# One running sum of probability tiles in the attention stage of a hybrid attention and recurrence layer

## The chip, the core and the metric

The kernel runs on one core of a Trainium2 chip. The metric is the device time of one execution in microseconds (us). The engines of the core work in parallel, each through its own instructions in a fixed order, and wait for one another by semaphores: TensorE (PE) multiplies matrices, VectorE (DVE), ScalarE (ACT) and GpSimd (POOL) work on elements, and SyncE (SP) issues the transfers between the memory outside the core and its own. SBUF is the memory on the core that all engines read. PSUM, in banks, takes what TensorE produces.

## The reference

One layer takes 2048 latent tokens of width 1024 and 256 context tokens. After a modulated RMS norm one projection feeds two groups of heads, whose outputs are concatenated and projected again; a SwiGLU feed-forward part follows. The change concerns the attention group alone:

```python
def latent_attention(qx, kx, vx, kc, vc):        # 8 query heads, 2 key/value heads, head_dim 64
    keys = jnp.concatenate([kc, kx], axis=1)     # 256 + 2048 = 2304 keys
    vals = jnp.concatenate([vc, vx], axis=1)
    def block(q):                                # 128 queries at a time
        s = jnp.einsum('bqkgd,bnkd->bkgqn', q, keys).astype(jnp.float32) * scale
        p = jax.nn.softmax(s, axis=-1)
        return jnp.einsum('bkgqn,bnkd->bqkgd', p.astype(vals.dtype), vals)
```

So for each query the kernel needs the largest score, the sum of the exponentials over 2304 keys, and the exponentials times the values. The other group is a gated linear recurrence over the same tokens.

## The kernel before

The program runs in stages: modulation and projections, then attention and recurrence together, the output projection, and the feed-forward part in two halves. The change touches the second of these.

**Items.** Attention is cut into 32 items (class `Item`): 16 blocks of 128 queries for each of the 2 key/value heads. An item holds 4 query heads of 128 queries, so 512 columns, against 18 key tiles of 128 keys (`NKT`). The loop over `x` counts key tiles of all items in turn: step `k` of item `n` is `x = 18 n + k`.

**A step** does three things. `scores` multiplies one key tile with the 512 query columns in two matrix products (lines 1096 and 1097: `qa` with the keys `K`, then a second one with the low parts and the maximum, `qb` with `KB`), and ScalarE writes the exponential into half of a pair tile `p` of 128 by 1024 (line 1100), so that an item has 9 pairs, 0 to 8. Beside it `chunk` works for the NEXT item: one more matrix product (`mx`, line 1065, or two halves at line 1071) whose row minima VectorE reduces into `mn` (lines 1067 and 1073). The score is kept negated, so the minimum gives the maximum. A bank for `mx` comes from a pool of two, `ps_mx`.

**The maxima.** After the last chunk VectorE reduces `mn` to `neg`, 128 by 4 (line 1077). At step 10 `maxima` transposes it on TensorE into a bank of `ps_mx` (`pn`, line 1082), ScalarE copies 4 rows of it, and they go into the next item's `qb`.

**The two events.** At step 10 (the first event, pairs 0 to 3) and at step 2 of the item after (the second event, pairs 4 to 8) TensorE leaves the scores and runs a batch: `pa`, the recurrence's products (line 724), and then `av`, values times exponentials (line 1121, column halves of 64). After that the sums over the keys are made: a pair of 128 by 1024 is multiplied with `one32`, 32 columns of ones, in 8 small matrix products (line 1129), which add up in columns 256 to 383 of `av`. A matrix product in float32 stands as two records in the trace, so 8 of them are 16 records. The banks of `av` are copied out at step 3 (`drain`), the sums inverted at step 10 (`invert`, line 1139) and applied at step 13 (`finish`, `pb` and `oo`).

**The sums.** Not every pair is multiplied with ones. A table `SUMS = ".PEP.PPE."` has a letter for each pair: a dot opens a group that is multiplied with ones, P is added to its group by GpSimd as soon as the pair is there, E is added by VectorE in the event. So pairs 0 to 3 become one tile `ps` in the first event, 4 to 7 another in the second, and pair 8 is multiplied by itself. An item has 4 additions on GpSimd, 2 on VectorE (all at line 1111) and 3 times 8 products with ones. The tile `ps` has one buffer (`op`, bufs=1).

**The recurrence** runs alongside. In each event, `rec.round()` yields the `pa` products and then one level of its work: VectorE's `copy_predicated` into `A` (line 737), ScalarE's `M`, GpSimd's `M`, `Q` and `C` (lines 753, 758 and 761). VectorE also makes the decay products `T` (line 779) after the event.

**The order.** In this stage TensorE, VectorE, ScalarE and GpSimd run in the order in which the code is written (`manual_schedule`); only SP's queue is left to the scheduler after the first item. A wait at the head of an engine therefore holds everything behind it.

## Time and profile before

| | us |
|---|---|
| median of 3 runs | 3124.36 |
| lowest and highest run | 3119.69, 3128.83 |
| span of the profiled execution | 3122.6 |
| stage of the items in it, from 731.51 to 1635.50 | 904.0 |
| mean granted TensorE clock | 0.996 |

A row of a timeline reads: start in us from the span's start, length in us, engine, line, operation, what it writes and reads, shape, number of instructions merged, and in brackets the engine's idle time before it with what ended it. A row of the chain of waits reads: start, length, engine, what, count; it is the work that the end hangs on. A row of groups reads: what, count | busy time, mean of one in ns | idle time before, by what ended it. Matrix products are pipelined and overlap in these rows, so the time that one costs is seen from the distance between starts. GpSimd's spans are rough.

### The profile page before, as it was taken

What the parts mean: (1) busy time and instruction counts of PE and PEld (TensorE: products, weight loads), DVE (VectorE), ACT (ScalarE), POOL (GpSimd) and SP (SyncE); (2) the same over time, 40 slices, a digit from 0 to 9 for tenths busy, and PEclk for the clock granted to TensorE, in tenths of its full rate; (3) what the DMA queues carried; (4) which work ended last, traced back from release to release, by engine and by line L of the source; (5) the groups of instructions that cost most, each with busy time, mean ns of one, the idle gap of its engine ahead of it and who ended that gap; (6) DMA issues with size and microseconds to landing.
All of it is one profiled execution on the core that took longest, in us unless ns stands there. A gap on an engine that the chain in (4) does not pass through costs nothing.

```text
span 3122.6 us, 51024 instructions
## 1 busy us (share of the span) xinstructions
PE 3069.2 (98%) x18732; PEld 2472.9 (79%) x18732; DVE 1863.3 (60%) x3234; ACT 1302.1 (42%) x2656; POOL 1647.5 (53%) x1302
## 2 busy tenths in 40 slices
PE   7999999999999999999999999999999999999998
PEld 5888888887777778777778878888878788888887
DVE  5554665526787786787745574544468844333567
ACT  4422332314455555455553243333345533333454
POOL 3422232205998888898862118776600177676122
PEclk9999999999999999999999999999999999999999
DMA  8343455425111222111124344656495533332755
GB/s 286 101 148 118 142 150 161 140 72 140 42 35 48 65 55 72 40 46 54 42 76 154 116 155 155 212 175 213 169 329 191 188 114 109 102 101 101 253 195 196
DMA packets 374789, 410.75 MB, mean 132 GB/s; under 512 B 36261, under 2 KB 265865, under 8 KB 374026
## 3 DMA queue, kind: packets, MB, share of 16 engines
q1 hardware_dynamic: 374538, 407.49, 40.9%
q8 instruction: 147, 2.41, 0.3%
q14 instruction: 104, 0.85, 0.1%
HBM read 277.54 MB, written 133.97 MB: 132 GB/s over the span
## 4 chain that ended last, share of the span: by engine, by line
PE 82%; DVE 6%; DMA 2%; POOL 2%; issue 1%; ACT 1%; SPq 0%; POOLq 0%; ACTq 0%; DVEq 0%
PE pA L1685 14%; PE pB L1685 7%; PE av L1121 7%; PE f L346 6%; PE y L1261 6%; PE pd0A L1982 4%; PE s L1096 3%; PE pC L1685 3%; PE pd1A L1982 3%; PE s L1097 3%; PE mx L1065 3%; DVE mn L1067 2%; PE i L353 2%; PE pd0B L1982 2%; PE pd1B L1982 2%; PE pa L724 2%
## 5 line engine op out<-in xcount | busy, mean ns | idle before, releaser
L1100 ACT ACTIVATE p<-s 128x512 f32<-128x512 f32 x576 | 337.8, 600 | 375.3 <-PE s L1097 361.4
L1067 DVE TENSOR_REDUCE mn<-mx 128x1 f32<-128x512 f32 x496 | 336.9, 689 | 176.4 <-PE mx L1065 173.7
L1121 PE MATMUL av<-p,VS 128*64 128x256 f32 x2304 | 259.9, 380 | 0.0
L1096 PE MATMUL s<-qa,K 128*128 128x512 f32 x576 | 244.7, 425 | 1.1 <-ACT p L1100 1.0
L1097 PE MATMUL s<-qb,KB 128*128 128x512 f32 x576 | 227.4, 395 | 0.0
L1121 PEld LDWEIGHTS av<-p,VS 128*64 128x64 f32 x2304 | 160.4, 137 | 75.2 <-issue 1.1
L1111 POOL TENSOR_TENSOR ps<-p,p 128x1024 f32<-128x1024 f32 x64 | 153.2, 2394 | 104.5 <-ACT p L1100 104.4
L1065 PE MATMUL mx<-K,qa 128*128 128x512 f32 x496 | 199.7, 403 | 2.7 <-DVE mn L1067 1.4
L346 PE MATMUL f<-hTh,wh 128*128 128x512 f32 (+1 forms) x640 | 187.8, 373 | 0.0
L1111 POOL TENSOR_TENSOR ps<-ps,p 128x1024 f32<-128x1024 f32 x64 | 153.0, 2391 | 11.9 <-ACT p L1100 10.6
L1919 DVE TENSOR_TENSOR dl<-dl,x 128x512 fp32r<-128x512 f32 x154 | 113.4, 760 | 68.1 <-ACT x L1912 63.9
L1912 ACT ACTIVATE x<-dl 128x512 fp32r<-128x512 f32 x154 | 96.2, 632 | 97.0 <-DMA dl<-s_hid0S 39.2
L758 POOL TENSOR_TENSOR Q<-Q,T 128x512 f32<-128x512 f32 x96 | 129.2, 1362 | 8.1 <-PE pa L724 7.7
L346 PEld LDWEIGHTS f<-hTh,wh 128*128 128x128 f32 x640 | 116.2, 189 | 20.0 <-DVE ge L361 0.2
L1912 ACT ACTIVATE dh<-dl 128x512 fp32r<-128x512 f32 x154 | 89.0, 624 | 101.5 <-PE pd1A L1982 44.7
L1919 DVE TENSOR_TENSOR dl<-dl,dh 128x512 fp32r<-128x512 f32 x154 | 105.5, 698 | 42.7 <-ACT dh L1912 40.4
L1096 PEld LDWEIGHTS s<-qa,K 128*128 128x128 f32 x576 | 109.3, 190 | 26.7 <-issue 12.3
L123 POOL TENSOR_TENSOR rs_xf<-ms_xf,mhalf 128x1 f32<-128x1 f32 x16 | 9.8, 617 | 223.5 <-DVE ms_xf L121 221.5
L1065 PEld LDWEIGHTS mx<-K,qa 128*128 128x128 f32 x496 | 93.7, 189 | 38.2 <-DVE mn L1067 15.3
L1097 PEld LDWEIGHTS s<-qb,KB 128*128 128x128 f32 x576 | 109.6, 190 | 14.8 <-issue 0.2
L346 PE MATMUL f<-hTl,wh 128*128 128x512 f32 (+1 forms) x320 | 118.0, 369 | 0.0
L1949 POOL TENSOR_TENSOR y<-y,yg 128x512 f32<-128x512 f32 x24 | 40.5, 1704 | 145.0 <-DVE yg L1948 118.0
(435 smaller groups left out, 8961.8 us busy)
## 6 DMA issues: line engine op xcount, KB each, us to landing
w<-in_w_gu_dram SPq DMA_DIRECT2D x88, 512.0 KB
wm<-in_w_mod_dram SPq DMA_DIRECT2D x24, 1024.0 KB
dl<-s_wT SPq DMA_DIRECT2D x88, 256.0 KB
dl<-s_wB SPq DMA_DIRECT2D x66, 256.0 KB
wq<-in_w_down_dram SPq DMA_DIRECT2D x44, 256.0 KB
s_wT<-wq SPq DMA_DIRECT2D x44, 256.0 KB
dl<-s_hid1S SPq DMA_DIRECT2D x44, 256.0 KB
dl<-s_hid0S SPq DMA_DIRECT2D x44, 256.0 KB
```

The source lines that it names most:

```text
L346: nc.tensor.matmul(pm[:, :n], w[wi][:, k, c0:c0 + P], hT[b][hi][:, k, :], start=(k == 0 and i == 0), stop=(k == KT - 1 and i == 2))
L1065: nc.tensor.matmul(s, self.qa[:, h * P:(h + 1) * P], K[:, k * 512:(k + 1) * 512], start=True, stop=True)
L1067: nc.vector.tensor_reduce(self.mn[:, h, k:k + 1], s, axis=AX.X, op=ALU.min)
L1096: nc.tensor.matmul(s, KS[self.g][:, ks], self.qa, start=True, stop=False)
L1097: nc.tensor.matmul(s, KB[k // 6][:, k % 6 * P:(k % 6 + 1) * P], self.qb, start=False, stop=True)
L1100: nc.scalar.activation(self.pairs[p][:, o:o + 512], s, AF.Exp, scale=-1.0)
L1111: (nc.gpsimd if SUMS[p] in "PQ" else nc.vector).tensor_tensor(t, a, self.pairs[p], op=ALU.add)
L1121: nc.tensor.matmul(self.av[i * 64:(i + 1) * 64, :256], VS[k // 6][:, k % 6, :], self.pairs[k // 2][:, o:o + 256], start=(k == 0), stop=(k ...
L1261: nc.tensor.matmul(py, m[:, k, :], wo[k][w][hf], start=(k == 0 and i == 0), stop=(k == KT - 1 and i == 2), skip_group_check=True)
L1685: nc.tensor.matmul(acc, w[wi][:, k, :], x[xi][k], start=(start and k == 0 and i == 0), stop=(stop and k == KH - 1 and i == 2), skip_group_ ...
L1919: nc.vector.tensor_tensor(lo, f32v(lo), f32v(hi), op=ALU.subtract)
L1982: nc.tensor.matmul(cur[t], l[:, t * P:(t + 1) * P], r, start=(start and j == 0 and f == 0), stop=(stop and j == NHF - 1 and f == 2), skip_ ...
```

## The change

`SUMS` and its groups go. An item has one tile `ps`, and every pair is added to it: pairs 1, 3, 5 and 6 by GpSimd when they are there (`POOL_ADDS`), pairs 2 and 4 by VectorE in the first event and 7 and 8 in the second (`DVE_ADDS`). The first of VectorE's two additions stands where its one stood, before the recurrence's level, the other after the level. The products with ones are made once per item, in the second event. GpSimd's addition of pair 5 now continues the sum that VectorE left, where it began a new tile before.

`neg` becomes one tile of 128 by 128 for all items, zero outside its first 4 columns, and all 128 columns are transposed. `smapad` takes the place in `sma` that the old `neg` tiles had.

```diff
--- before.py
+++ after.py
@@ -620,6 +620,7 @@
         kvp = pool(st, "kvp", 1, side="right")
         qpl = pool(st, "qpl", 1, side="right")
         sm = pool(st, "sma", 3, side="right")
+        sm.tile([P, 24], F32, name="smapad", bufs=1)
         pp = pool(st, "pp", 8, side="right")
         op = pool(st, "op", 1, side="right")
         ps_st = pool(st, "ps_st", 3, PSUM, side="right")
@@ -1041,7 +1042,7 @@
             def __init__(self, n, qt, g):
                 self.n, self.qt, self.g = n, qt, g
                 self.nm = f"{qt}_{g}"
-                self.pairs, self.sums, self.av = {}, {}, None
+                self.pairs, self.sum, self.av = {}, None, None
 
             def load(self):
                 self.qa = qpl.tile([P, 512], F32R, tag="qa", name=f"qa{self.nm}", bufs=3)
@@ -1073,13 +1074,12 @@
                     nc.vector.tensor_reduce(self.mn[:, h:h + 2, 4], s.rearrange("p (h k) -> p h k", h=2),
                                             axis=AX.X, op=ALU.min)
                 if c == 17:
-                    self.neg = sm.tile([P, 4], F32, tag="neg", name=f"neg{self.nm}")
-                    nc.vector.tensor_reduce(self.neg, self.mn, axis=AX.X, op=ALU.min)
+                    nc.vector.tensor_reduce(neg[:, :4], self.mn, axis=AX.X, op=ALU.min)
 
             def maxima(self):
 
                 pm = ps_mx.tile([P, 512], F32, tag="x", name=f"pn{self.nm}")
-                nc.tensor.transpose(pm[:4, :P], self.neg, ident)
+                nc.tensor.transpose(pm[:, :P], neg, ident)
                 mr = sm.tile([4, P], F32R, tag="mr", name=f"mr{self.nm}", bufs=2)
                 nc.scalar.activation(mr, pm[:4, :P], AF.Copy)
                 for h in range(4):
@@ -1098,17 +1098,15 @@
                                  start=False, stop=True)
                 o = k % 2 * 512
                 nc.scalar.activation(self.pairs[p][:, o:o + 512], s, AF.Exp, scale=-1.0)
-                if k % 2 and SUMS[p] in "PD":
-                    later(ADD[SUMS[p]], self.add, p)
-
-            def add(self, p):
-
-                g = SUMS.rindex(".", 0, p)
-                t = a = self.sums.get(g)
-                if t is None:
-                    a, t = self.pairs[g], op.tile([P, 1024], F32, tag="ps", name=f"ps{self.nm}_{g}")
-                    self.sums[g] = t
-                (nc.gpsimd if SUMS[p] in "PQ" else nc.vector).tensor_tensor(t, a, self.pairs[p], op=ALU.add)
+                if k % 2 and p in POOL_ADDS:
+                    self.add(p, nc.gpsimd)
+
+            def add(self, p, eng):
+
+                a = self.sum
+                if a is None:
+                    a, self.sum = self.pairs[0], op.tile([P, 1024], F32, tag="ps", name=f"ps{self.nm}")
+                eng.tensor_tensor(self.sum, a, self.pairs[p], op=ALU.add)
 
             def products(self, b):
 
@@ -1122,13 +1120,11 @@
                                          VS[k // 6][:, k % 6, :],
                                          self.pairs[k // 2][:, o:o + 256],
                                          start=(k == 0), stop=(k == NKT - 1), skip_group_check=True)
-                for p in [p for p in range(k0 // 2, k1 // 2) if SUMS[p] == "."]:
-                    t = self.sums.get(p, self.pairs[p])
-                    for o in range(0, 1024, 512):
-                        for i in range(4):
-                            nc.tensor.matmul(self.av[i * 32:(i + 1) * 32, 256:384], one32,
-                                             t[:, o + i * P:o + (i + 1) * P], start=False,
-                                             stop=(p == SUMS.rindex(".") and o > 0), skip_group_check=True)
+                for o in range(0, 1024, 512) if k1 == NKT else ():
+                    for i in range(4):
+                        nc.tensor.matmul(self.av[i * 32:(i + 1) * 32, 256:384], one32,
+                                         self.sum[:, o + i * P:o + (i + 1) * P], start=False, stop=o > 0,
+                                         skip_group_check=True)
 
             def drain(self):
                 self.ot = op.tile([P, 384], F32, tag="ot", name=f"ot{self.nm}")
@@ -1148,11 +1144,13 @@
                 nc.sync.dma_start(s_att[self.g][:, self.qt * P:(self.qt + 1) * P].rearrange("(e p) t -> p e t", p=P),
                                   oo.rearrange("p (e t) -> p e t", e=2))
 
-        SUMS, ADD = ".PEP.PPE.", {'P': 0, 'D': 1}
+        POOL_ADDS, DVE_ADDS = (1, 3, 5, 6), [[2, 4], [7, 8]]
         KS = [kvp.tile([P, NTOK], F32R, name=f"K{g}") for g in range(2)]
         KB = [kvp.tile([P, NTOK // 3], F32R, name=f"KB{r}") for r in range(3)]
         VS = [kvp.tile([P, 6, 64], F32, name=f"VS{r}") for r in range(3)]
         QB = [qpl.tile([P, 512], F32R, name=f"qb{i}") for i in range(2)]
+        neg = kvp.tile([P, P], F32, name="neg")
+        nc.gpsimd.memset(neg, 0.0)
         one32 = kvp.tile([P, 32], F32, name="one32")
         nc.gpsimd.memset(one32, 1.0)
         pick = kvp.tile([P, 2, P], F32, name="pick")
@@ -1320,9 +1318,8 @@
                         gate1 = [f32v(free.pop(0)) for _ in range(2)]
                         for hf in range(2):
                             nc.sync.dma_start(gate1[hf], rows_bcast(modrow[0, 2 * D + hf * 512:2 * D + hf * 512 + 512]))
-                for p in range(BATCHES[-1][0] // 2, BATCHES[-1][1] // 2):
-                    if SUMS[p] in "EQ":
-                        items[-1].add(p)
+                for p in DVE_ADDS[-1]:
+                    items[-1].add(p, nc.vector)
                 items[-1].products(len(BATCHES) - 1)
                 items[-1].drain()
                 items[-1].invert()
@@ -1391,11 +1388,10 @@
                     continue
                 made = rec.round() if e in ROUNDS else iter(())
                 next(made, 0)
-                for p in range(BATCHES[e][0] // 2, BATCHES[e][1] // 2):
-                    if SUMS[p] in "EQ":
-                        items[m].add(p)
+                items[m].add(DVE_ADDS[e][0], nc.vector)
+                next(made, 0)
+                items[m].add(DVE_ADDS[e][1], nc.vector)
                 items[m].products(e)
-                next(made, 0)
                 for ahead, u in rec.decays(x) if e == TE else ():
                     u.extend(min(ahead, 7))
                 if TE == 9 and e in ROUNDS:
```

VectorE at the first event of one item, before: the inversion of the item before, the addition of pair 2, the level's two copies, the decays, and the first minimum after the event. In these names `p_0_2` is pair 2 of the item and `mx_0_3` chunk 3 of the next.

```order
L1139 RECIPROCAL ot_0_9020<-ot_0_9020 128x128
L1111 TENSOR_TENSOR ps_0_0_9018<-ps_0_0_9018,p_0_2_9026 128x1024
L737 COPY_PREDICATED A_8343<-mask,pa_9098 128x512
L737 COPY_PREDICATED A_8840<-mask,pa_9098 128x512
L779 TENSOR_REDUCE T_4_9153<-T_3_9012 128x32
L779 TENSOR_REDUCE T_1_9155<-T_0_8904 128x256
L1067 TENSOR_REDUCE mn_0_9069<-mx_0_3_9163 128x1
```

```order
L1135 RECIPROCAL ot_0_8927<-ot_0_8927 128x128
L1109 TENSOR_TENSOR ps_0_8925<-ps_0_8925,p_0_2_8933 128x1024
L738 COPY_PREDICATED A_8282<-mask,pa_9004 128x512
L738 COPY_PREDICATED A_8754<-mask,pa_9004 128x512
L1109 TENSOR_TENSOR ps_0_8925<-ps_0_8925,p_0_4_8970 128x1024
L780 TENSOR_REDUCE T_4_9052<-T_3_8919 128x32
L780 TENSOR_REDUCE T_1_9054<-T_0_8818 128x256
L1068 TENSOR_REDUCE mn_0_8975<-mx_0_3_9061 128x1
```

The addition of pair 4 has come in between the level's copies and the decays, ahead of the first minimum that TensorE's bank waits for.

VectorE at the second event of the same item, before and with the change.

```order
L1067 TENSOR_REDUCE mn_0_9069<-mx_0_12_9238 128x1
L1111 TENSOR_TENSOR ps_0_4_9161<-ps_0_4_9161,p_0_7_9188 128x1024
L737 COPY_PREDICATED A_8343<-mask,pa_9241 128x512
L737 COPY_PREDICATED A_8840<-mask,pa_9241 128x512
L779 TENSOR_REDUCE T_5_9307<-T_4_9153 128x16
L779 TENSOR_REDUCE T_2_9309<-T_1_9155 128x128
L1067 TENSOR_REDUCE mn_0_9069<-mx_0_13_9319 128x1
```

```order
L1068 TENSOR_REDUCE mn_0_8975<-mx_0_12_9136 128x1
L1109 TENSOR_TENSOR ps_0_8925<-ps_0_8925,p_0_7_9086 128x1024
L738 COPY_PREDICATED A_8282<-mask,pa_9139 128x512
L738 COPY_PREDICATED A_8754<-mask,pa_9139 128x512
L1109 TENSOR_TENSOR ps_0_8925<-ps_0_8925,p_0_8_9101 128x1024
L780 TENSOR_REDUCE T_5_9198<-T_4_9052 128x16
L780 TENSOR_REDUCE T_2_9200<-T_1_9054 128x128
L1068 TENSOR_REDUCE mn_0_8975<-mx_0_13_9210 128x1
```

The addition of pair 8 stands behind the level's copies, and the tile that it completes is the one that TensorE multiplies with ones.

TensorE at the second event of that item, before and with the change, up to the first score after it.

```order
L724 MATMUL pa_9241<-Q_8344,M_5_9142 64x64 x8
L724 MATMUL pa_9241<-Q_8841,M_2_9144 64x64 x8
L1121 MATMUL av_0_9116<-p_0_4_9064,VS_7038 64x256 x4
L1121 MATMUL av_0_9116<-p_0_5_9081,VS_7038 64x256 x4
L1121 MATMUL av_0_9116<-p_0_6_9166,VS_7039 64x256 x4
L1121 MATMUL av_0_9116<-p_0_7_9188,VS_7039 64x256 x4
L1121 MATMUL av_0_9116<-p_0_8_9203,VS_7039 64x256 x4
L1129 MATMUL av_0_9116<-ps_0_4_9161,one_7042 32x128 x8
L1129 MATMUL av_0_9116<-p_0_8_9203,one_7042 32x128 x8
L1096 MATMUL s_0_3_9311<-qa_0_8705,K_7032 128x512
```

```order
L725 MATMUL pa_9139<-Q_8283,M_5_9023 64x64 x8
L725 MATMUL pa_9139<-Q_8755,M_2_9025 64x64 x8
L1119 MATMUL av_0_9035<-p_0_4_8970,VS_7039 64x256 x4
L1119 MATMUL av_0_9035<-p_0_5_8987,VS_7039 64x256 x4
L1119 MATMUL av_0_9035<-p_0_6_9064,VS_7040 64x256 x4
L1119 MATMUL av_0_9035<-p_0_7_9086,VS_7040 64x256 x4
L1119 MATMUL av_0_9035<-p_0_8_9101,VS_7040 64x256 x4
L1125 MATMUL av_0_9035<-ps_0_8925,one_7045 32x128 x8
L1096 MATMUL s_0_3_9202<-qa_0_8628,K_7033 128x512
```

One of two groups of 8 products with ones is gone here. At the first event the one group that stood behind `av` is gone, and no other row of TensorE has moved. GpSimd's and ScalarE's rows of this stage stand in the same order as before.

## The prediction

> **What bounds the kernel now.** I read the engines' busy time first, then the window of 206 us in the middle of the item stage, seven items long, after which the rows repeat (columns: length, then busy us of PE, PEld, DVE, ACT, POOL, then clock, DMA share and GB/s), and then the chain of waits from 900 to 1000 us.
>
> ```profile
> PE 3069.2 (98%) x18732; PEld 2472.9 (79%) x18732; DVE 1863.3 (60%) x3234; ACT 1302.1 (42%) x2656; POOL 1647.5 (53%) x1302
> ```
>
> ```profile
> 836.00:1042.00 206.00, 204.20 (x1954) 157.35 (x1953) 157.09 (x258) 108.75 (x254) 182.53 (x151) 1.00 0.19 52
> ```
>
> ```profile
> by line: PE av L1121 19.9%; PE s L1096 11.6%; PE mx L1065 10.3%; PE s L1097 10.1%; PE pa L724 5.6%; DVE mn L1067 5.5%; PE av L1129 5.3%; DVE ps L1111 5.0%; PE psb L828 3.1%; POOL ps L1111 2.4%; POOL M L753 2.3%; POOL Q L758 2.3%; issue 2.1%
> ...
> 904.22 1.08 PE pa L724 x32
> 905.30 4.32 PE av L1121 x40
> 909.62 1.01 PE av L1129 x32
> ...
> 916.50 0.27 PE pn L1082
> 916.77 1.08 PE pa L724 x32
> 917.86 3.46 PE av L1121 x32
> 921.31 0.57 PE av L1129 x16
> ```
>
> TensorE sets the time here: it is busy 204.2 of 206 us. But GpSimd has 182.5 and VectorE 157.1, and both stand in the chain (`DVE mn`, `DVE ps`, `POOL`). So a product saved on TensorE counts in full only where VectorE and GpSimd are not late. The first three rows of times are a second event of an item, the last three a first event, with the transpose of `neg` (`pn`) ahead of it.
>
> **What goes.** From these rows, 16 records with ones take 0.57 us in a first event, and the second event goes from 1.01 to 0.57, which is 0.44. Per item that is 1.01 us, for 32 items **−32 us**. That TensorE has this on its own path is plain: no other engine appears between `av` and the next score.
>
> **What comes.** VectorE makes 64 more additions, and the place decides what they cost. Its rows around the two events:
>
> ```profile
> 904.86 1.22 DVE L1111 TENSOR_TENSOR ps<-ps,p 128x1024 f32<-128x1024 f32 x1
> 905.99 1.36 DVE L737 COPY_PREDICATED A<-mask,pa 128x512 f32<-128x512 int32 x2
> 911.56 2.08 DVE L1067 TENSOR_REDUCE mn<-mx 128x1 f32<-128x512 f32 x3 [3.81 <-PE mx L1065]
> ...
> 917.91 1.61 DVE L1111 TENSOR_TENSOR ps<-ps,p 128x1024 f32<-128x1024 f32 x1
> 919.45 1.36 DVE L737 COPY_PREDICATED A<-mask,pa 128x512 f32<-128x512 int32 x2
> 920.69 0.27 DVE L779 TENSOR_REDUCE T<-T 128x64 f32<-128x128 f32 x1
> 922.82 2.07 DVE L1067 TENSOR_REDUCE mn<-mx 128x1 f32<-128x512 f32 x3 [1.85 <-PE mx L1065]
> ```
>
> The 64 additions of now, in ns from shortest over the median to longest:
>
> ```profile
> L1111 DVE TENSOR_TENSOR ps<-ps,p x64: 1159/1491/5865, 732.3 to 1628.9; 128x1024 f32<-128x1024 f32 x64
> ```
>
> So one more costs between 1.2 and 5.9 us. I take the median, 1.5, and treat the long ones by themselves.
>
> *First event.* VectorE is idle 1.85 us here before the first minimum. The event is 0.57 shorter now, so 1.28 of that is left for an addition of 1.5. VectorE would be 0.22 late. TensorE bears about 0.2 of lateness, because two banks hold minima: `mx` starts 0.69 apart from one step to the next, as long as a reduction of 0.69 (2.07 for 3), and only the third `mx` needs the first bank. What goes beyond that TensorE waits for, and everything behind `mx` on it, the scores and so ScalarE's exponentials, waits too. The stall is therefore 1.5 + 0.57 − 0.2 = 1.87 less the idle time. The other six first events of the 206 us have these idle times in the bracket:
>
> ```profile
> 843.57 0.69 DVE L1067 TENSOR_REDUCE mn<-mx 128x1 f32<-128x512 f32 x1 [0.81 <-PE mx L1065]
> ...
> 869.40 2.08 DVE L1067 TENSOR_REDUCE mn<-mx 128x1 f32<-128x512 f32 x3 [2.19 <-PE mx L1065]
> ...
> 897.54 2.07 DVE L1067 TENSOR_REDUCE mn<-mx 128x1 f32<-128x512 f32 x3 [1.16 <-PE mx L1065]
> ...
> 952.17 0.69 DVE L1067 TENSOR_REDUCE mn<-mx 128x1 f32<-128x512 f32 x1 [1.42 <-PE mx L1065]
> ...
> 981.29 0.69 DVE L1067 TENSOR_REDUCE mn<-mx 128x1 f32<-128x512 f32 x1 [1.14 <-PE mx L1065]
> ...
> 1017.24 1.38 DVE L1067 TENSOR_REDUCE mn<-mx 128x1 f32<-128x512 f32 x2 [1.52 <-PE mx L1065]
> ```
>
> That gives stalls of 1.06, 0, 0.71, 0.02, 0.45, 0.73 and 0.35, together 3.3 us in seven items, and for 32 items (times 32/7) **+15 us**. So the first event gives back nearly all of its 18 us. With additions of 1.2 the stalls are 1.8 in seven items and +8 us; with 1.8 they are 5.1 and +23.
>
> *Second event.* The products with ones now need pair 8 in the sum, so TensorE may wait at them, and everything behind. At 904.86 nothing happens: the copies end at 905.99 + 1.36 = 907.35, a second addition at 908.9, and `av` ends at 909.62. VectorE's idle time of 3.81 takes the addition afterwards. Two other rows of the seven are tighter:
>
> ```profile
> 880.30 1.78 DVE L1111 TENSOR_TENSOR ps<-ps,p 128x1024 f32<-128x1024 f32 x1
> 882.01 1.37 DVE L737 COPY_PREDICATED A<-mask,pa 128x512 f32<-128x512 int32 x2
> ...
> 933.85 4.97 DVE L1111 TENSOR_TENSOR ps<-ps,p 128x1024 f32<-128x1024 f32 x1
> 938.75 1.37 DVE L737 COPY_PREDICATED A<-mask,pa 128x512 f32<-128x512 int32 x2
> ```
>
> ```profile
> 884.24 0.64 PE L1129 MATMUL av<-ps,one 128*32 128x128 f32 x16
> ...
> 938.88 0.65 PE L1129 MATMUL av<-ps,one 128*32 128x128 f32 x16 [1.16 <-DVE ps L1111]
> ```
>
> At 880.30 the second addition ends at 883.4 + 1.5 = 884.9, some 0.6 after TensorE gets to the ones. At 933.85 VectorE's addition took 4.97 us and TensorE waits 1.16 already; with the copies and another addition it waits 1.3 + 1.5 = 2.8 more. Together 3.4 in seven items, **+16 us** in all.
>
> *Why an addition takes 4.97.* GpSimd at that place:
>
> ```profile
> 933.30 1.84 POOL L758 TENSOR_TENSOR Q<-Q,F 128x512 f32<-128x512 f32 x1
> 935.05 1.12 POOL L758 TENSOR_TENSOR Q<-Q,T 128x512 f32<-128x512 f32 x1
> 936.09 1.06 POOL L761 TENSOR_TENSOR C<-M,F 128x256 f32<-128x256 f32 x1
> 937.05 0.69 POOL L761 TENSOR_TENSOR C<-M,T 128x256 f32<-128x256 f32 x1
> ```
>
> VectorE's addition ends one addition's length after GpSimd's last `C` (937.74), so it was held back until GpSimd was idle. Two more are like it:
>
> ```profile
> 1139.60 4.97 DVE L1111 TENSOR_TENSOR ps<-ps,p 128x1024 f32<-128x1024 f32 x1
> 1370.39 5.87 DVE L1111 TENSOR_TENSOR ps<-ps,p 128x1024 f32<-128x1024 f32 x1
> ```
>
> All others end by 2.81, between two of GpSimd's instructions. I read this as a race that VectorE can lose in any event: 3 of 64. If the 64 new ones lose as often, three more are lost. What a loss costs, GpSimd's rows at the first event of 917.91 show:
>
> ```profile
> 918.40 3.09 POOL L758 TENSOR_TENSOR Q<-Q,T 128x512 f32<-128x512 f32 x2
> 921.45 1.25 POOL L761 TENSOR_TENSOR C<-M,T 128x256 f32<-128x256 f32 x2
> ```
>
> `C` ends at 922.7, an addition held back until then at 923.9, where it would else end at 919.45 + 1.36 + 1.5 = 922.3: 1.6 late, and GpSimd can't go on holding it back, because its next addition needs this one. Three times 1.6 is 5; one in a second event costs less, so **+4 us**, between 0 and, at three times the rate, 14.
>
> The Trainium skill ("SBUF — State Buffer", section "SBUF: two separate sides") says that the two engines share a port pair as an exclusive lock, which whoever starts first holds for its instruction. By that rule an addition would wait for one GpSimd instruction at most, and this term would be 0 and the sum 4 us lower. The row with 4.97 us, in which four GpSimd instructions ran first, speaks against taking the rule alone.
>
> *The rest.* GpSimd is held up as well. The two `Q` of 918.40, unhindered 1.12 each, take 3.09 beside the addition. That is 0.85 per addition, 12 us more in seven items, where it had 23.5 idle (206 less 182.5). I count it as hidden in that idle time: 0 us; the upper end stands with the rivals. Pair 5's addition on GpSimd now waits for VectorE's pair 4, but stands behind its `M`, `Q` and `C`, of which the two `Q` alone last 3.09.
>
> The transpose of `neg` waits for VectorE, not for its own width:
>
> ```profile
> PEld pn L1082 <- DVE mn L1067: 8.8, 22, 0.4
> ```
>
> In 22 of 31 items that wait comes ahead of it, so I take 0, with ±8 us as bounds: its own 0.27 us at 916.50, gone or doubled, 31 times.
>
> **The sum.** −32 + 15 + 16 + 4 = **+3 us** on an execution of 3122.6, so 3125.6. The median of the runs shown is 1.8 above that execution, so I say **3127**. I forecast no change that can be told: 0.3%, or 9 us, is about what a measurement of this kernel can distinguish from none.
>
> **The rivals.**
>
> *Faster: VectorE has room.* The additions last 1.2, as at 904.86, and the lost races at 933.85 and its like vanish because all phases shift. Then −32 + 8 in the first events, + 3 in the second ones (0.6 in seven items, at 880.30), no new losses: −21, with the same 1.8 **3103**. For it speaks that the bad row comes at one place of the 206 us and depends on a few hundredths of a us. Against it: in the first event the new addition falls amid GpSimd's `Q`, where the rows show 1.6 to 1.8.
>
> *Slower: lost races.* The new addition in a first event stands where GpSimd works without a pause, so it may lose as a rule. It is then late until GpSimd has ended `C`, 1.6 us each time. With half of the 32 lost that is 26 in place of the 4, so 3125.6 + 22 + 1.8 = **3149**. It decides from about four beyond the three that the sum holds. For it: 4.97 us where GpSimd ran four instructions in a row. Against it: no first event shows a lost race now.
>
> *Slower: GpSimd becomes the bound.* With 194.5 of 206 us busy its slack is small, and it lies behind the second event, while pairs 5 and 6 and the level follow the first with hardly a gap. Pair 3 would then come late to VectorE's pair 2 at the next first event. Fully exposed, two times 0.85 per item, 1.7 us, is 54; half of it gives 3127 + 27 = **3154**. It decides when more than a tenth is exposed. Against it: VectorE waits for GpSimd's addition four times only, for 6.3 us in all:
>
> ```profile
> DVE ps L1111 <- POOL ps L1111: 6.3, 4, 2.5
> ```
>
> **Chances.** The forecast, 3127, has 0.42, with a range of its own of 3118 to 3133. Faster has 0.31, lost races 0.16, GpSimd 0.11. The range goes from 3099, which takes in most of the faster case, to 3150: lost races in their size. So faster by over 0.3% is 0.31, within 0.42, slower 0.27.
>
> **What will show it.** Right: TensorE's group with ones falls from 1536 records to 512, the bracket before the first minimum after a first event is near 0 in most of the items, and TensorE then waits for `DVE mn` about half a us per item; the ones wait for `DVE ps` in the second events at the places of 880 and 933. Wrong in the first event: brackets of 0.5 and more there, hence a gain. Wrong by lost races: more than ten additions of VectorE above 3 us. Wrong by GpSimd: `DVE ps` waiting for `POOL ps` far beyond four times, and GpSimd with less than 10 us idle in seven items. The clock, 1.00 in these windows, should stay.

## The result, and the profile after

The change makes the kernel slower by about half a per cent. The median is 3139.28 us (five runs, 3133.76 to 3147.88) against 3127.65 us for the kernel before in the same session (five runs, 3119.69 to 3132.04). The ratio is 1.0046, with a 95% interval of 1.0027 to 1.0064: 11.6 us more, where I forecast +3 and called it no change. The profiled executions differ by nearly as much: a span of 3133.7 us against 3122.6. Of the five runs of the change the longest has the lowest mean granted clock, 0.991, and the two shortest have 0.994 and 0.995; the profiled run before has 0.996.

First the row of the busy time of the engines, after the change (busy us, share of the span, instructions).

```profile
PE 3047.9 (97%) x17708; PEld 2448.9 (78%) x17708; DVE 1963.7 (63%) x3298; ACT 1302.8 (42%) x2656; POOL 1697.6 (54%) x1303
```

TensorE has lost 1024 records and 21 us of work, VectorE has gained 64 instructions and 100 us, GpSimd 50 us although its instructions are the same but for one. The difference lies in the item stage. These are the windows of the item stage (length, then busy us of PE, PEld, DVE, ACT, POOL, clock, DMA share, GB/s), before:

```profile
731.50:1635.50 904.00, 895.71 (x8462) 684.01 (x8463) 673.74 (x1088) 475.18 (x1081) 776.25 (x619) 1.00 0.20 56
```

and after:

```profile
730.00:1650.00 920.00, 877.01 (x7438) 661.32 (x7438) 772.94 (x1152) 475.70 (x1080) 826.71 (x619) 0.99 0.19 55
```

Before, TensorE was idle for 8.3 us of the stage (904.0 less 895.7). Now it is idle for 43. The stage is 16 us longer; outside it this execution happens to be 5 us shorter, in work that the change doesn't touch. So that +11 us of the spans fit the +11.6 of the medians is in part luck.

What TensorE waits for is in the waits of that stage (who waited, for whom: us in all, times, longest). A product and its weight load can wait for the same thing at once, so rows of PE and PEld overlap. Before:

```profile
PEld mx L1065 <- DVE mn L1067: 10.6, 38, 0.6
...
PEld av L1129 <- DVE ps L1111: 5.3, 4, 1.6
PE av L1129 <- DVE ps L1111: 3.5, 3, 1.2
```

After:

```profile
PEld mx L1066 <- DVE mn L1068: 36.7, 56, 5.8
PEld av L1125 <- DVE ps L1109: 26.4, 17, 4.5
PE mx L1066 <- DVE mn L1068: 19.4, 14, 5.4
PE av L1125 <- DVE ps L1109: 19.1, 9, 4.1
...
PEld pn L1082 <- DVE mn L1068: 8.8, 22, 0.4
DVE T L780 <- POOL C L762: 5.9, 4, 1.7
DVE ps L1109 <- POOL ps L1109: 5.4, 4, 2.3
```

Both waits that the prediction names have grown: the minima behind a first event (`mx` for `mn`), and the ones in a second event (`av` for `ps`). VectorE's wait for GpSimd's additions is as rare as before, 4 times. The transpose waits exactly as before, 8.8 us in 22 items.

Of the tile of sums these are the rows that matter (shortest, median and longest in ns):

```profile
L1125 PE MATMUL av<-ps,one x512: 272/273/422, 749.5 to 1649.7; 128*32 128x128 f32 x171
L1109 DVE TENSOR_TENSOR ps<-ps,p x128: 1160/1514/6905, 730.7 to 1647.2; 128x1024 f32<-128x1024 f32 x128
```

To see where the 16 us come from I cut the stage of each trace at TensorE's own instructions into 64 events and the 64 stretches behind them. An event runs from its first `pn` or `pa` to the first score behind it, a stretch from there to the next event. Every piece is compared with the same piece of the kernel before. The sums, in us:

| kernel | first events | behind them | second events | behind them | stage | at half clock |
|---|---|---|---|---|---|---|
| the change | −17.1 | +28.2 | +2.6 | +2.5 | +16.2 | 13.7 |
| the change, a second run | −17.1 | +24.5 | −0.3 | +4.2 | +11.3 | 20.5 |

The last column is the time in the stage for which the trace's clock records give TensorE half its clock (0.50); before, it is 0.

**A first event with its stall.** VectorE and then TensorE behind the event whose idle bracket was 0.81 us before:

```profile
842.85 2.17 DVE L1109 TENSOR_TENSOR ps<-ps,p 128x1024 f32<-128x1024 f32 x1
844.94 0.21 DVE L780 TENSOR_REDUCE T<-T 128x32 f32<-128x64 f32 x1
845.07 1.21 DVE L780 TENSOR_REDUCE T<-F 128x512 f32<-128x1024 f32 x1
846.20 0.68 DVE L1068 TENSOR_REDUCE mn<-mx 128x1 f32<-128x512 f32 x1
```

```profile
846.93 0.50 PE L1066 MATMUL mx<-K,qa 128*128 128x512 f32 x1 [1.37 <-DVE mn L1068]
```

The minimum has no bracket any more: VectorE comes straight from the addition and the decays. TensorE, which got two `mx` ahead, stands still until the minimum has freed a bank. The addition took 2.17 us, not the 1.5 that I had put in.

**A second event with its wait,** at the place of 880:

```profile
882.01 1.82 DVE L1109 TENSOR_TENSOR ps<-ps,p 128x1024 f32<-128x1024 f32 x1
883.75 1.35 DVE L738 COPY_PREDICATED A<-mask,pa 128x512 f32<-128x512 int32 x2
884.99 2.62 DVE L1109 TENSOR_TENSOR ps<-ps,p 128x1024 f32<-128x1024 f32 x1
```

```profile
887.67 0.64 PE L1125 MATMUL av<-ps,one 128*32 128x128 f32 x16 [1.65 <-DVE ps L1109]
```

Here too the order of things is as forecast, and the addition of pair 8 is 1.1 us longer than the 1.5 assumed. The wait is 1.65 where 0.6 was forecast.

**A held-up addition,** at the place of 933: VectorE, GpSimd beside it, and TensorE behind it.

```profile
936.81 5.56 DVE L1109 TENSOR_TENSOR ps<-ps,p 128x1024 f32<-128x1024 f32 x1
942.30 1.31 DVE L738 COPY_PREDICATED A<-mask,pa 128x512 f32<-128x512 int32 x2
943.51 1.20 DVE L1109 TENSOR_TENSOR ps<-ps,p 128x1024 f32<-128x1024 f32 x1
```

```profile
936.85 1.80 POOL L759 TENSOR_TENSOR Q<-Q,F 128x512 f32<-128x512 f32 x1
938.62 1.07 POOL L759 TENSOR_TENSOR Q<-Q,T 128x512 f32<-128x512 f32 x1
939.65 1.04 POOL L762 TENSOR_TENSOR C<-M,F 128x256 f32<-128x256 f32 x1
940.66 0.63 POOL L762 TENSOR_TENSOR C<-M,T 128x256 f32<-128x256 f32 x1
```

```profile
944.77 0.43 PE L1125 MATMUL av<-ps,one 128*32 128x128 f32 x8 [4.08 <-DVE ps L1109]
```

GpSimd goes through all its queued instructions, and VectorE's addition ends 1.08 us after the last of them (942.37 less 941.29). Before the change TensorE waited 1.16 us for such an addition. Now the copies and another addition stand between it and the ones, and it waits 4.08.

**What follows such a wait.** By the clock records of the trace TensorE's granted clock is 0.50, half of full, for 3.41 us from 946.06 on. Here are two windows of the same length behind the wait (the clock is the figure after POOL's), and products in each of them:

```profile
946.10:949.40 3.30, 3.30 (x9) 2.52 (x8) 1.79 (x3) 2.17 (x4) 2.37 (x1) 0.50 0.00 0
949.60:952.90 3.30, 3.21 (x17) 2.36 (x15) 2.96 (x7) 2.84 (x6) 1.71 (x1) 1.00 0.00 0
```

```profile
946.62 0.63 PE L1097 MATMUL s<-qb,KB 128*128 128x512 f32 x1
947.04 0.63 PE L1066 MATMUL mx<-K,qa 128*128 128x512 f32 x1
...
949.78 0.39 PE L1096 MATMUL s<-qa,K 128*128 128x512 f32 x1
950.02 0.40 PE L1097 MATMUL s<-qb,KB 128*128 128x512 f32 x1
```

In the first window there are 9 products, 0.42 us from start to start, in the second 17, at 0.24. The change has four such stretches in this stage, at 792, 946, 1154 and 1479; its second run has four as well, two of them of 6.83 us. The price shows in the stretches of work behind second events, where nearly all pieces without half clock are within 0.05 us of the kernel before: in the kernels that keep the banks and the place of the ones, eight pieces hold a whole stretch of 3.41 us, and these are 1.5 to 1.6 us longer. Four times that, some 6 us of the stage, is an estimate for the change.

In the 13 traces of this document there are 38 such stretches in this stage. Each starts within 5.4 us of the beginning of a TensorE wait of 1.4 us or more. The kernel before, and the one below without both additions, have no wait of TensorE over 1.2 us here and no half clock. Which wait brings one isn't settled: one of 2.06 us, at 1149 in the second run, brings none.

### The profile page after: what moved, and what is told of

Read it like the earlier page. It is cut to its first block, busy times and chain, and to the rows that moved or that the text cites. A ratio compares the mean times of both kernels' runs of the same rounds, so it can differ in the third digit from the quotient of the medians.

```text
span 3133.7 us, 49101 instructions
## 1 busy us (share of the span) xinstructions
PE 3047.9 (97%) x17708; PEld 2448.9 (78%) x17708; DVE 1963.7 (63%) x3298; ACT 1302.8 (42%) x2656; POOL 1697.6 (54%) x1303
## 4 chain that ended last, share of the span: by engine, by line
PE 82%; DVE 9%; POOL 3%; DMA 2%; issue 2%; ACT 1%; SPq 1%; POOLq 0%; ACTq 0%; DVEq 0%
PE pA L1681 15%; PE pB L1681 7%; PE f L346 6%; PE y L1259 5%; PE av L1119 5%; PE pd0A L1978 4%; PE pC L1681 3%; PE s L1096 3%; PE pd1A L1978 3%; PE mx L1066 3%; PE hq L346 3%; PE s L1097 3%; DVE mn L1068 2%; PE i L353 2%; PE q L353 2%
## 5 line engine op out<-in xcount | busy, mean ns | idle before, releaser
L1109 POOL TENSOR_TENSOR ps<-ps,p 128x1024 f32<-128x1024 f32 x96 | 229.8, 2394 | 28.3 <-ACT p L1100 18.7
L1109 DVE TENSOR_TENSOR ps<-ps,p 128x1024 f32<-128x1024 f32 x128 | 217.3, 1698 | 6.0 <-POOL ps L1109 5.4
L759 POOL TENSOR_TENSOR Q<-Q,T 128x512 f32<-128x512 f32 x96 | 155.9, 1639 | 9.9 <-PE pa L725 9.9
```

What stands on the lines that cost most here:

```text
L1109: eng.tensor_tensor(self.sum, a, self.pairs[p], op=ALU.add)
```

## The experiments

The theory is that of the prediction: the price is VectorE's lateness at two points, the first minimum behind a first event and the ones in a second event. It stands against three others: that the 128-wide transpose costs the time, that VectorE's additions and GpSimd hinder each other (held-up additions, GpSimd late), and that GpSimd has become the bound. No kernel here changes the clock by itself; its share is read from the last column. Each kernel was compared piece by piece as above; the sums:

| kernel | first events | behind them | second events | behind them | stage | at half clock |
|---|---|---|---|---|---|---|
| wide transpose alone | +5.0 | +0.4 | +0.1 | +0.1 | +5.5 | 3.4 |
| without the addition of pair 4 | −17.1 | +1.8 | +7.5 | +5.9 | −1.9 | 13.7 |
| without the addition of pair 8 | −17.1 | +22.3 | −15.8 | +1.7 | −9.0 | 3.4 |
| without both | −17.1 | +2.2 | −16.4 | 0.0 | −31.3 | 0 |
| reductions in their place | −17.1 | +6.4 | −3.2 | +3.6 | −10.3 | 10.2 |
| three banks for minima, two for scores | −18.0 | +25.3 | −2.7 | +11.7 | +16.2 | 6.8 |
| pair 4 in the second event, pair 8 by itself | −17.1 | +2.2 | +4.5 | +3.4 | −7.1 | 6.8 |
| the same with the other banks | −18.0 | +11.6 | +7.7 | +14.3 | +15.5 | 13.7 |
| pairs 4, 7, 8 in the second event, ones later | −17.1 | +8.3 | −33.9 | +77.7 | +35.0 | 30.7 |
| pair 4 added by GpSimd | −17.1 | +53.0 | +3.7 | +0.2 | +39.8 | 20.5 |

**Each addition by itself.** Three kernels leave out the addition of pair 4, of pair 8, and both. In these, and in the kernel with reductions below, the copy of `av` out of its banks also adds 1, in the same instruction.

```diff
-                items[m].add(DVE_ADDS[e][1], nc.vector)
+                if e:                      # without pair 4; "if not e" without pair 8
+                    items[m].add(DVE_ADDS[e][1], nc.vector)
```

> The changed kernel without VectorE's addition of pair 4 in the first event (pair 4 is left out of the sums, and 1 is added to what is copied out of av so that no sum is zero). Compared by the length of the item stage, which grew from 904 to 920 us with the change: first events -17, the steps behind them +28, second events +3, the steps behind them +2. Theory (the addition makes VectorE late behind the first event, and TensorE waits for it): the +28 go to under 3, the first events stay at -17 and the second events at about +5, so the stage is 9 us shorter than before, 25 shorter than with the change. Rival (GpSimd, held up by all of the additions, is late for the level and for pair 3): at least half of the +28 stays.

> The changed kernel without VectorE's addition of pair 8 in the second event (pair 8 is left out of the sums, and 1 is added to what is copied out of av). Theory (the ones wait for that addition in some of the second events): second events go from +3 to about -12, with a wait left where the addition of pair 7 is held up for about 5 us, and the steps behind the first events stay at +28 within 5. Stage about 0 against before. Rival (GpSimd is freed too by one addition less and the steps behind the first events get better with it): these fall to under 20.

> The changed kernel without both of VectorE's new additions (pairs 4 and 8 are left out of the sums, and 1 is added to what is copied out of av). What the products with ones alone are worth: theory, -32 us of the stage (0.57 and 0.44 per item), and at most 5 given back where an addition is held up. Rival (the saved time of TensorE is not on the path, because VectorE's minima set the pace anyway): under 16 us are gained.

Measured in one run each, beside 3123.31 us for the kernel before: 3125.93 without pair 4, 3115.66 without pair 8, 3092.36 without both. So the work saved on TensorE is worth 31 us, when nothing is in its way; the sum had −32. The addition of pair 4 by itself brings back 22.3 us of stage (−9.0 less −31.3), 20.1 of them behind the first events. That of pair 8 brings back 29.4 (−1.9 less −31.3), 23.9 of them in the second events. The waits of the stage without pair 8 and without pair 4 show one of the two each. Without pair 8:

```profile
PEld mx L1066 <- DVE mn L1068: 34.4, 59, 2.3
...
PE mx L1066 <- DVE mn L1068: 16.2, 16, 1.9
```

and without pair 4:

```profile
PEld av L1125 <- DVE ps L1109: 31.7, 18, 4.1
PE av L1125 <- DVE ps L1109: 23.7, 14, 3.7
...
PEld mx L1066 <- DVE mn L1068: 12.6, 39, 1.1
```

The two costs together would be 51.7 us over the kernel without both. The change itself has 47.5 and, in its second run, 42.6. They needn't add exactly, because the long additions fall in other places each time (4 in the kernel without pair 4, 1 without pair 8, 3 and 2 in the two runs of the change), and with them the half clock. Without pair 4 that is most of why the stage is 1.9 us shorter than before and not the 9 expected: the 5.9 us behind its second events lie almost wholly in four stretches at half clock.

**The transpose.** The kernel before, with the 128-wide tile and its transpose alone.

```diff
-                    self.neg = sm.tile([P, 4], F32, tag="neg", name=f"neg{self.nm}")
-                    nc.vector.tensor_reduce(self.neg, self.mn, axis=AX.X, op=ALU.min)
+                    nc.vector.tensor_reduce(neg[:, :4], self.mn, axis=AX.X, op=ALU.min)
...
-                nc.tensor.transpose(pm[:4, :P], self.neg, ident)
+                nc.tensor.transpose(pm[:, :P], neg, ident)
```

> The kernel before with only the transpose of the maxima made from the zeroed 128-wide tile. Theory: no change, 0 within 2 us of the item stage, since the transpose waits for VectorE's minima in most items. Rival (a transposition of 4 columns costs TensorE a change of its layout before and after): 3 to 8 us shorter.

Measured: a median of 3123.86 us against 3122.31, ratio 1.0003 (0.9994 to 1.0013). The transpose costs nothing that can be told. Of the +5.5 us in its trace 4.4 are a single held-up addition of 6.8 us in one first event, with 3.4 us at half clock behind it; most other first events are 0.06 longer.

**Reductions in place of the two additions.** They read a pair of the same size and write one column of the sum, so VectorE stays occupied, by an instruction with one input in place of two.

```diff
-                items[m].add(DVE_ADDS[e][1], nc.vector)
+                items[m].stand_in(DVE_ADDS[e][1])
...
+            def stand_in(self, p):
+                nc.vector.tensor_reduce(self.sum[:, 0:1], self.pairs[p], axis=AX.X, op=ALU.add)
```

> The changed kernel with a reduction of the pair (128 by 1024, one input) in the place of each of VectorE's two new additions, so that VectorE is as busy but reads one tile of SBUF instead of two (pairs 4 and 8 are left out of the sums, and 1 is added to what is copied out of av). Theory 1 (what costs is that VectorE's additions and GpSimd hold one another up): reductions of 1.2 us each, none longer than 1.5, the steps behind the first events at about +8 to +12 instead of +28, second events near -8, stage -15 to -10 against before. Theory 2 (what costs is VectorE's own time, whatever it reads): the steps behind the first events stay at +20 or more, and the stage is longer than before.

Measured: 3110.73 us beside 3123.31. The rows of its tile, the additions that are left and the reductions:

```profile
L1109 DVE TENSOR_TENSOR ps<-ps,p x64: 1159/1457/5869, 731.5 to 1619.0; 128x1024 f32<-128x1024 f32 x64
L1113 DVE TENSOR_REDUCE ps<-p x64: 1193/1204/1227, 732.8 to 1621.4; 128x1 f32<-128x1024 f32 x64
```

All 64 reductions last between 1.19 and 1.23 us, in the same places, amid the same work of GpSimd, where an addition that is not held up lasts 1.16 to 3.1. Behind the first events the stall falls from +28.2 to +6.4, in the second events from +2.6 to −3.2. So of what the two additions cost over the kernel without both (47.5 us, or 42.6) about half, 21.0 us, is there with reductions too. Of these, 11 are two held-up additions of the old kind, in items 15 and 26, with the half clock behind them, and some 10 are what work of 1.2 us in these places costs. The other half is gone, and with it what differs: the longer times of a second addition with two inputs beside GpSimd. The cleanest comparison is behind the first events with the kernel without pair 8, since neither has a held-up addition or half clock there: over the kernel without both, the addition of pair 4 costs 20.1 us, a reduction 4.2. This doesn't part VectorE's share from GpSimd's, whose `Q` are shorter too (1.32 us in the mean with reductions, 1.64 in the change). The Trainium skill ("SBUF — State Buffer", section "Who interferes with whom") says that a VectorE instruction with at most one input in SBUF doesn't contend with GpSimd, outside certain two-port modes, and one with two inputs does, with a GpSimd instruction that reads SBUF. The two rows agree: 1.19 to 1.23 us against up to 5.87.

**The banks.** The stall behind a first event starts when TensorE has filled both banks for minima. A third bank, taken from the scores, gives it one more step.

```diff
-        ps_st = pool(st, "ps_st", 3, PSUM, side="right")
+        ps_st = pool(st, "ps_st", 2, PSUM, side="right")
+        ps_m3 = pool(st, "ps_m3", 1, PSUM, side="right")
...
-                s = ps_mx.tile([P, 512], F32, tag="x", name=f"mx{self.nm}_{c}")
+                s = (ps_m3 if (self.n * 19 + c + (c > 2)) % 3 == 2 else ps_mx).tile([P, 512], F32, tag="x", name=f"mx{self.nm}_{c}")
```

> The changed kernel with three banks for the minima instead of two, taken from the scores, which keep two. Tests the step that TensorE bears only 0.2 us of VectorE's lateness because the third mx needs the first bank. Theory: with one bank more it bears 0.7 us more, so the steps behind the first events cost about 16 us less than the 20 that they cost without a long addition: stage 10 to 16 us shorter than with the change, if two banks for the scores cost nothing. Rival (VectorE's minima pace these steps anyway and the lateness comes back at the next wait): these steps stay within 5 us.

> The version with pair 4 at the head of the second event and pair 8 by itself, with three banks for the minima and two for the scores. Theory: the transpose no longer waits for a bank (about 0.25 us per item) and the steps ahead of the first events get shorter by up to 8 us in all, nothing else changes: median near 3105. Rival (with two banks the scores wait for ScalarE's exponentials, 0.60 us against 0.69 per step): the same or slower than that version.

Measured: 3138.94 us in one run; in the same session the median of the kernel before is 3125.14 and a second run of the change 3132.88. With pair 4 moved (below), the same banks give a median of 3128.78, ratio 1.0016 (1.0000 to 1.0031), where that kernel has 0.997 without them. The waits of the first of these kernels:

```profile
PEld s L1097 <- ACT p L1101: 60.0, 173, 1.4
...
PEld mx L1067 <- DVE mn L1069: 13.6, 24, 1.6
```

The wait for the minima falls from 36.7 to 13.6 us, so it is indeed the bank that passes VectorE's lateness on to TensorE. But the scores, with two banks, now wait for ScalarE's exponentials: 60 us in 173 places, where the change has 5.3 us in 12. The gain is spent there: behind the first events 3 us are saved (+25.3 after +28.2) where 16 were expected, and the stage has the same +16.2.

**The addition of pair 4 where VectorE has room.** VectorE's idle time lies in the events, while TensorE runs its batch: the second event at 904.22, in the rows of the prediction, lasts 6.4 us, and VectorE's addition and copies there 2.5. Here pair 4 is added in the second event ahead of the level, with pair 7, and pair 8 keeps its own products with ones. So an item has 3 additions on VectorE and 16 products with ones, 8 fewer than before.

```diff
-        POOL_ADDS, DVE_ADDS = (1, 3, 5, 6), [[2, 4], [7, 8]]
+        POOL_ADDS, DVE_ADDS = (1, 3, 5, 6), [[2], [4, 7]]
...
-                for o in range(0, 1024, 512) if k1 == NKT else ():
-                    for i in range(4):
+                for t in (self.pairs[8], self.sum) if k1 == NKT else ():
+                    for o in range(0, 1024, 512):
+                        for i in range(4):
...
-                items[m].add(DVE_ADDS[e][0], nc.vector)
-                next(made, 0)
-                items[m].add(DVE_ADDS[e][1], nc.vector)
+                for p in DVE_ADDS[e]:
+                    items[m].add(p, nc.vector)
+                next(made, 0)
```

> One running sum, but with VectorE's addition of pair 4 at the head of the second event, ahead of pair 7 and of the level's copies, and pair 8 multiplied with ones by itself, ahead of the sum: no new addition in the first event, where VectorE has little idle time, one in the second, where it has 3.8 us. Theory: 16 products with ones less per pair of events than... that is 8 less per item than before, -18 us; no stall behind the first event; second events 0 within 0.2 except where an addition is held up, +4. So the stage is 14 us shorter than before and the median near 3112. Rival (two additions in a row are held up by GpSimd more often): 4 us shorter or none.

Measured: a median of 3112.91 us (six runs) against 3122.31, ratio 0.997 (0.9958 to 0.9982). It beats both kernels. Its waits in the stage:

```profile
PEld mx L1066 <- DVE mn L1068: 13.3, 41, 1.1
...
PEld av L1126 <- DVE ps L1109: 8.7, 9, 2.4
```

The wait for the minima is as without both additions (13.1), and the whole saving of the first events, 17.1 us, less 2.2, is kept. In most of its second events the piece is 0.0 longer. Its price is in a few: two held-up additions cost 3.9 us each with what follows them, of which 1.55 are the half clock behind.

**Everything in the second event, the ones a step later.** Pairs 4, 7 and 8 are all added there, and the ones wait until the step in which `av` is copied out, so that 8 products with ones are enough.

```diff
-        POOL_ADDS, DVE_ADDS = (1, 3, 5, 6), [[2, 4], [7, 8]]
+        POOL_ADDS, DVE_ADDS = (1, 3, 5, 6), [[2], [4, 7, 8]]
...
             if k == 3 and n:
+                items[n - 1].ones()
                 items[n - 1].drain()
```

> One running sum with pairs 4, 7 and 8 all added by VectorE in the second event, and the products with ones (8 per item) one step later, behind the next score, with the copy out of av behind them. Theory: -32 us for the products, +6 for two more changes of TensorE's layout (0.2 per item), and VectorE late by about 0.7 us behind the second event, +22: stage -4, within 8. Rival (VectorE's 3.8 us of idle time behind the second event take both additions): -20 or better.

Measured: a median of 3141.49 us, ratio 1.0068 (1.0048 to 1.0087). The ones wait all the more, and now with the scores of the next steps behind them:

```profile
PEld av L1128 <- DVE ps L1109: 54.2, 30, 4.6
...
PE av L1128 <- DVE ps L1109: 41.2, 27, 4.1
...
POOL ps L1109 <- PE av L1128: 27.7, 16, 6.1
```

The last row is a new wait: `ps` has one buffer, and the next item's sum can't begin before the late ones have read it. A third addition, behind the copies, is more than a second event hides here. The stage, expected 4 us shorter, is 35 longer in the traced execution, which is the longest of the four (3154.72 us) and has 30.7 us at half clock.

**GpSimd adds pair 4.** The same as two kernels above, with the addition of pair 4 on GpSimd.

```diff
-        POOL_ADDS, DVE_ADDS = (1, 3, 5, 6), [[2], [4, 7]]
+        POOL_ADDS, DVE_ADDS = (1, 3, 4, 5, 6), [[2], [7]]
```

> The version with pair 8 by itself, but pair 4 added by GpSimd instead of VectorE: five additions on GpSimd per item, two on VectorE as before. Tests how much room GpSimd has: it gets 2.4 us more per item of 29, with 3.4 idle before. Theory (its idle time lies behind the second event and cannot be used ahead of the first): the level and pairs 5 and 6 come late, VectorE waits for GpSimd's sums: slower than before by 10 to 40 us. Rival (GpSimd has room): as short as with pair 4 in the second event, near 3113, or better since VectorE has nothing new.

Measured: a median of 3169.58 us, ratio 1.0142 (1.0117 to 1.0166). One wait of the stage shows why:

```profile
DVE ps L1109 <- POOL ps L1109: 59.5, 33, 4.4
```

So this is what GpSimd as the bound looks like: VectorE waits for GpSimd's additions 33 times, 59.5 us, and the stretches behind the first events grow by 53, some 9 of them by 20.5 us at half clock (at 1.55 for 3.41, an estimate). In the change the same wait is 5.4 us, 4 times. That rival is out for the change, and close: 32 additions on GpSimd bring it about.

**The change once more,** to see what differs from run to run.

> The changed kernel once more, to see what repeats between executions. Theory: stalls behind the first events and waits of the ones repeat within 0.1 us at each place, and only the additions of about 5 to 7 us change in number and place, always the first addition of an event, none of the new ones behind the level's copies. Rival (the new additions are held up that long as well in another execution): at least one of the long ones is an addition of pair 4 or 8.

Measured: 3132.88 us; pieces in the first table. The stalls behind the first events of items 4 to 10 repeat to 0.02 us: 1.75, 0.07, 1.14, 0.32, 1.52, −0.01 and 0.80, after 1.74, 0.06, 1.15, 0.30, 1.50, −0.03 and 0.80. What differs most is which additions are held up: three in the first run (at 936.8, 1146.7 and 1467.5), two in the second (881.7 and 1297.4). The half clock differs with them: the stretches at 946 and 1154 are gone, and two of 6.83 us, at 888 and 1304, have come; item 2 and item 25 have one in both runs.

## Where the prediction was right and where it was wrong

The mechanism was right, and nearly every place that it named. But terms of the sum were too small, and one was missing: the clock. The forecast was +3 us, no change that can be told, and the stage shows +16.2 and +11.3. The result lies inside the range, but that says little: at 51 us it took in all but one of the values named. Slower had 0.27.

- **What goes, −32.** Right. Without both additions the events save 33.5 us, 17.1 in the first and 16.4 in the second, and the whole kernel 31.
- **The first events, +15: mis-sized, +20.** Six of the seven brackets are gone as forecast, and TensorE waits. The rule (1.5 + 0.57 − 0.2, less the idle time) gave 3.3 us in seven items. Measured are 5.5, and 5.0 without the 0.5 of item 8 that is there with neither addition. What failed is one duration for every place. The 1.5 was right as a median: the 32 additions of pair 4 have 1.51. But in the seven places they last 2.17, 1.51, 2.11, 1.86, 1.21, 1.22 and 1.51 us, and two of the long ones fall where the idle time was short (0.81 and 1.16). With these the rule gives 1.73, 0, 1.32 and 0.38 for the first four, and measured are 1.74, 0.06, 1.15 and 0.30. For the last three it gives 0.16, 0.45 and 0.36, and measured are 1.50, −0.03 and 0.80; the first of these has the cause below, the other two I didn't follow further. The bound that the prediction gave for additions of 1.8 us, +23, was somewhat nearer, and the text had its reason: the rows of 1.6 to 1.8 amid GpSimd's `Q`. The factor 32/7 was too large, which offset part of the miss: items 28 to 31 have 0.3 us between them. In the change itself 26.0 stand here and not 20, because of one held-up addition (4.9) and half clock in item 2 (1.6).
- **GpSimd is hidden, 0: wrong in one item of seven.** In item 8 the decays wait for GpSimd. Its `Q` beside the addition last 3.33 us for two, `C` is late by that, and VectorE's `T` needs `C` and stands ahead of the next minima. VectorE and GpSimd there:

```profile
957.00 1.21 DVE L1109 TENSOR_TENSOR ps<-ps,p 128x1024 f32<-128x1024 f32 x1
...
961.24 0.69 DVE L780 TENSOR_REDUCE T<-F 128x256 f32<-128x512 f32 x1 [1.74 <-POOL C L762]
```

```profile
957.07 3.33 POOL L759 TENSOR_TENSOR Q<-Q,T 128x512 f32<-128x512 f32 x2
960.35 0.85 POOL L762 TENSOR_TENSOR C<-M,T 128x256 f32<-128x256 f32 x1
```

  The prediction asked only whether GpSimd has idle time in seven items, not who waits for its last instruction. With items 15 and 22 this is 3 times about 1 us.
- **The second events, +16: mis-sized, +20.3 and +21.5** in the two runs, with what stands behind them (held-up additions and half clock among it). The places are right. At 880 the price is 1.7 and not 0.6, again because the addition lasts 2.62 us; it repeats every seven items, and in both runs wherever no addition is held up. At 933 the forecast of 2.8 more is about right where VectorE's first addition is held up (2.9 more, then 1.6 behind, which is the half clock), and wrong where it isn't: there the event is 1.45 shorter than before.
- **Lost races, +4: the count was wrong one way, the price the other.** I let the new additions lose as often as the old. They never do: in the 13 traces 39 of 1216 additions last over 3.2 us, all 39 are the first of their event, and none of the 384 that stand behind another is among them. But the price of one, 1.6 in the text, is 3.3 to 5.5 us, taken from pieces that have one in one run of the change and none in the other, because the copies, a second addition and the ones stand behind it, and because TensorE's longer wait is followed by half clock, 1.6 us of the 5.5 at 946. One of them, 6.91 us in a first event, costs 4.9 against the same item without the addition of pair 8, half clock included.
- **The clock, taken to stay at 1.00: wrong.** The prediction gave it no term. The stage has 13.7 us at half clock in the change and 20.5 in its second run, where the kernel before has none. At 1.5 to 1.6 us for each 3.41 that is some 6 us of the 47.5 that the change costs over the kernel without both additions (an estimate). Item 2 shows it in one place: with the same wait of TensorE, 1.94 and 1.91 us, the stretch is 3.82 us longer than before in the change, with half clock, and 2.21 without pair 8, where there is none.
- **The transpose, 0.** Right, by the kernel with it alone.
- **The rivals.** GpSimd as the bound is out. Faster was wrong, since both of its conditions failed. Of lost races neither was as put: there are three in all, as before, where the rival needed about seven new ones, and one costs two to three and a half times the 1.6.

Put together over the kernel without both: −33.5 + 2.2 that is there in any case + 26.0 behind the first events + 21.5 in and behind the second = +16.2. Of the last two terms some 6 are half clock. What isn't settled is why an addition that comes first in its event can be passed by up to seven of GpSimd's instructions, and which event it strikes; that the second one never is may lie in how little GpSimd has left by then, which no run here tests.

## What to carry to other kernels

Before moving work to an engine with spare time on average, go place by place: take the idle time there, and a range of durations from rows beside what will run there. A stall is what is left over, so a median that is right on the whole (1.5 us assumed, 1.51 found in the first events) still gives too little when the long ones, here 2.1 to 2.2, fall where idle time is short. Put the new work where the engine is idle while the bound engine is occupied (here the head of the longer batch) and not between that and the first result that the bound engine waits for. And where two engines hinder each other, ask what stands behind the longest case: in a second event the same held-up addition cost 1.2 us before the change and 3.3 to 5.5 after it. And where the bound engine is made to wait, look at its clock behind the wait: a stall can cost more than its own length.

## What was not expected of the hardware

- A VectorE addition with both inputs in SBUF can be held up behind 2 to 7 of GpSimd's instructions in a row, for 3.8 to 6.9 us; between 3.1 and 3.8 us there is none among the 1216. Each of the 39 ends 1.08 or 1.09 us after the last of those instructions. A rule by which the loser waits for one instruction, which the prediction weighed, does not give these lengths.
- More additions do not clearly bring more of them: 3 of 64 before, 3 and 2 of 128 in the change, and between 1 and 5 in the other kernels, of 64 to 128.
- A reduction of the same size, with one input, is not lengthened in any of 64 places: 1.19 to 1.23 us.
- TensorE waits of 1.4 to 5.4 us can be followed by 3.41 or 6.83 us at half clock, 38 times in this stage over the 13 traces; 3.41 us of it cost 1.5 to 1.6.
- GpSimd pays as well: its 96 longer `Q` take 1.64 us each in the mean, 1.36 before, with not one more instruction in them. The groups of the stage (busy us, mean of one in ns, idle time before), before and after:

```profile
L758 POOL TENSOR_TENSOR Q<-Q,T 128x512 f32<-128x512 f32 x96 | 129.2, 1362 | 8.1 <-PE pa L724 7.7
```

```profile
L759 POOL TENSOR_TENSOR Q<-Q,T 128x512 f32<-128x512 f32 x96 | 155.9, 1639 | 9.9 <-PE pa L725 9.9
```
